# Second feed-forward of a two-layer step: the half products of the down projection woven in a written order, its sums in a place of their own

## The chip, the cores and the metric

The kernel runs on one core of a Trainium2 chip. The metric is the device time of one execution in microseconds (us). Before the change it was 1540.76 us, the median of three runs (1539.7 to 1543.07). One further execution was recorded by the hardware profiler: it took 1538.41 us, of which the instructions span 1536.6 us. All readings of the trace below are of that execution.

Engines are named as the profile names them: PE is the matrix engine, PEld its weight loads, DVE, ACT and POOL the vector, scalar and GpSimd engines, SP the engine that issues most loads.

## The reference, cut to what matters

The program computes one step through two trunk layers on 640 tokens (512 latent, 128 context) of width 1024. Layer 0 mixes the tokens by neighbourhood attention, layer 1 by a gated linear recurrent unit; each is followed by a SwiGLU feed-forward, and every part adds its result to the residual x through a gate vector:

```python
def _swiglu(x, w_gu, w_down):
    gate, up = jnp.split(x @ w_gu, 2, axis=-1)
    return (jax.nn.silu(gate) * up) @ w_down
```

The change lies in the second of the two feed-forwards. There `x @ w_gu` gives 22 units of 128 gate and 128 up columns (the hidden width is 2816), and `w_down` takes the 2816 hidden values back to eight rows of 128. Everything is float32.

## The kernel before, in words

**Arithmetic.** A float32 product is made of three matmuls on rounded halves: high weight by high data, high weight by low data, low weight by high data (lines 1208 to 1210 in `product`, 258 to 260 in `chunk`). So every weight tile and every data tile exists as a high part, cast by ACT (line 1668), and a low part, subtracted by DVE (line 1669). A matmul here is 128x128 by 128x320, since the 640 tokens are taken in two halves of 320 columns.

**Seven products in place of eight.** The second feed-forward treats a pair of output rows and the two halves of the tokens as a 2x2 block product and makes it from seven half products: A11·B11, A12·B21, S2·T2, S1·T1, S3·T3, A22·T4 and S4·B22. A are blocks of the weights, S sums of such blocks, B blocks of the data and T sums of those. Several products add up in one PSUM bank, one after the other: A11·B11, then S2·T2, S3·T3 and A22·T4 go into one bank ("mx"), S1·T1 and S4·B22 into a second ("mc" or "at"), A12·B21 has a third ("mm"). Between two products on a bank its value is copied out to SBUF by ACT, because it is a partial result that another output needs: this copy is called a snapshot ("snap", line 1214 for the gate products, line 1316 for the down products, where it also scales by the gate vector). PE can't write the next product into the bank until the snapshot is read out.

**Stages.** `ffn_halves` goes through the units of the hidden width. Two are plain and their down projection is done by `project_first` (96 matmuls, eight rows of 640 tokens, scaled into the tile of x and added to the residual in DRAM by eight POOL transfers of 320 KB that add in memory). The other 20 go in five chunks of four. A unit's gate and up columns are one pair of seven products, 84 matmuls, in `pair_a` (A11·B11, A12·B21), `pair_b` (S2·T2, S1·T1, S3·T3) and `pair_c` (A22·T4, S4·B22). DVE then multiplies gate and up and `hidden_sums` makes the data blocks B11, B21, B22 and T1 to T4 of the down product from the hidden values; part of them lies in a wide tile ("big"), part in the tile of x. After each of the first four chunks follows `down`: four pairs of output rows, seven products of six matmuls each, 168 matmuls. Its 16 results per chunk are 128x320 pieces of 160 KB, added to the residual in DRAM by POOL transfers (`add_x`); they are written into four places in SBUF (two called "sq", one "ssq", one "dg"), in turn. The last chunk is projected by `project_last`, after the residual is loaded back, and the final norm follows.

**Weights.** `down_weights` loads one pair's block, casts and subtracts the high and low parts, makes S1 to S4 on DVE (line 1298) in one of two places called "sum", and splits those too. POOL makes the same sums of the gate weights (line 1179) in the same two places. Weight halves are "whi"/"wlo" (from A) and "whx"/"wlx" (from S), three places of each.

**What sets the order.** Inside this feed-forward the order on each engine is made by a scheduler, which simulates the program and takes what it holds to be ready first; each instruction then waits for its inputs and for the places it writes. `in_order` (line 1672) pins engines to the order in which the code is written; before the change the second feed-forward doesn't use it. `ORDERED[:1]` is PE alone.

Of the kernel before, what the change touches and what calls it, by code (L numbers as in the profile page):

```python
# [50 lines left out]
PS = 4  # L51
BLK = ((0, 0), (0, 1), (1, 1), (1, 0))
# [90 lines left out]

class _Step:
    def __init__(self, ctx, nc, tc, i, o):
# [3 lines left out]
        self.n, self.ng, self.nu, self.hold, self.late = 0, 0, 0, None, []  # L149
# [491 lines left out]
    def project_last(self, w, hi, lo, gk):  # L641
# [26 lines left out]
        def square(f):  # L668
            q[f] = self.ssq[:, b0:b1] if f == 0 else self.t([P, HT], F32, "snap", 3, self.sb)[:, 0:b1 - b0]
            nc.scalar.activation(q[f], x[:, f, b0:b1], AF.Square)  # L670
# [14 lines left out]
        def final(k0, k1, t0, t1, r):  # L685
            v = x[:, k0:k1, t0:t1]
            nc.vector.tensor_tensor(v, v, r.unsqueeze(1).broadcast_to([P, k1 - k0, t1 - t0]), ALU.mult)
            nc.sync.dma_start(self.o["y"][k0 * P:k1 * P, t0:t1].rearrange("(k p) t -> p k t", p=P), v)
# [523 lines left out]
    def snap(self, ps):  # L1212
        s = self.t([P, HT], F32, "snap", 3, self.sb)
# [16 lines left out]
    def lay_hidden(self):  # L1230
        x = self.t([P, KT, NTOK], F32R, "x", 1, self.xp).rearrange("p k t -> p (k t)")
# [3 lines left out]
        spots += [(x, c * n) for c in range(6)] + [(t, c * n) for c in range(2) for t in self.wide]  # L1235
# [34 lines left out]

    def project_first(self, w, gk, xd):
        nc = self.nc
        G = self.need(self.gcols, gk)
        x = self.t([P, KT, NTOK], F32, "x", 1, self.xp)
        for f in range(0, KT, 2):
            for j, u in enumerate(self.two(w[f:f + 2], False)):
                o = x[:, f + j]
                for t0, t1 in CH:
                    ps = self.chunk(u, self.hhi, self.hlo, t0, t1, False)
                    for s, a, b in _pieces(t0, t1):  # L1280
                        g = G[:, s, f + j:f + j + 1]
                        if t0:
                            nc.vector.tensor_scalar(o[:, a:b], ps[:, a - t0:b - t0], g, None, ALU.mult)
                        else:
                            nc.scalar.activation(o[:, a:b], ps[:, a - t0:b - t0], AF.Copy, scale=g)
                self.add_x(xd, f + j, 0, o)

    def down_weights(self, i, d):
# [5 lines left out]
        s = self.t([P, 4, PS // 2 * P], F32, "sum", 2, self.sb)  # L1294
# [10 lines left out]
    def down(self, i, gk, xd):  # L1305
        nc, H = self.nc, self.H
        G = self.need(self.gcols, gk)
        W, b, c, u2, turn = {}, {}, {}, {}, count()

        def out():  # L1310
            tag = ("sq", "ssq", "sq", "dg")[next(turn) % 4]
            return self.t([P, HT], F32, tag, 1 + (tag == "sq"), self.sb)
# [6 lines left out]
        def snap(ps, f, t0):  # L1319
            return scaled(self.t([P, HT], F32, "snap", 3, self.sb), ps, f, t0)  # L1320
# [498 lines left out]
```

## Time and profile before

| what | us |
|---|---|
| median of three runs | 1540.76 |
| profiled execution | 1538.41 |
| span of its instructions | 1536.6 |
| PE busy in the span | 1485.3 (97%) |
| DVE busy | 1138.3 (74%) |
| ACT busy | 789.4 (51%) |
| POOL busy | 310.9 (20%) |
| start of the second feed-forward, two plain units and first chunk | 1057.0 to 1148.5 |
| first, second, third and fourth `down` | 1148.5 to 1187.8, 1238.3 to 1278.0, 1328.5 to 1369.0, 1419.7 to 1460.0 |

The profile counts PE as busy from a matmul's issue to its modelled end, at whatever clock was granted, so a high share does not say that PE ran at its full rate. The rate is seen from the number of matmuls in a stretch. The view of stretches prints for each stretch its length, then busy us and instruction count of PE, PEld, DVE, ACT and POOL, the granted PE clock as a share of the full one, the busy share of the DMA engines and GB/s. The view of waits lists whom an engine waited for, the total, the number of times and the longest time. In a timeline the bracket at a row's end gives the engine's idle time before it and what ended it.

### The profile page before, as it was taken

The page shows a single profiled execution, that of the slowest core. Times are in us where ns is not written, and L with a number is a line of the kernel's source. Part 1 is how long each engine was busy: PE and PEld are TensorE (multiplying, and loading weights), DVE is VectorE, ACT ScalarE, POOL GpSimd, SP SyncE. Part 2 cuts the span into 40 slices and gives each one's busy share as a digit, 9 for nine tenths or more (in the row PEclk, how much of TensorE's full clock was granted, in tenths as well). Part 3 has the DMA queues.
Part 4 walks back from the last instruction along what each step waited for, and adds up shares of the span by engine and source line. Part 5 has one row for each costly group of instructions (what it writes and reads, how often), then busy time and mean ns, then how long its engine had stood idle before and what let it go on. Part 6 is the DMA issues. An engine that isn't in the chain of part 4 may idle for free.

```text
span 1536.6 us, 26655 instructions
## 1 busy us (share of the span) xinstructions
PE 1485.3 (97%) x10281; PEld 1436.7 (93%) x10281; DVE 1138.3 (74%) x2166; ACT 789.4 (51%) x1489; POOL 310.9 (20%) x397
## 2 busy tenths in 40 slices
PE   9999999999999999999999999999988989898897
PEld 5999999899999999999999999999988979788797
DVE  6778787875777789878864799858684866759465
ACT  5667666754343244223343788646454544445454
POOL 0100000000022322112100011120515335152421
PEclk9999999999999999999999999999999999899999
DMA  9555555252478999778746442571636263453641
GB/s 359 187 164 168 150 165 167 68 192 83 137 241 318 343 345 333 254 248 269 257 144 203 169 152 96 209 244 56 138 106 100 83 118 89 115 91 101 107 149 69
DMA packets 94287, 268.50 MB, mean 175 GB/s; under 512 B 10144, under 2 KB 30800, under 8 KB 94032
## 3 DMA queue, kind: packets, MB, share of 16 engines
q1 hardware_dynamic: 57040, 157.06, 30.6%
q0 software_dynamic: 36944, 109.60, 24.8%
q8 instruction: 81, 1.33, 0.3%
q14 instruction: 46, 0.38, 0.1%
q10 hardware_dynamic: 176, 0.13, 0.0%
HBM read 206.18 MB, written 56.64 MB: 171 GB/s over the span
## 4 chain that ended last, share of the span: by engine, by line
PE 78%; DVE 7%; DMA 6%; ACT 4%; issue 2%; POOL 2%; DVEq 0%; SPq 0%; POOLq 0%; ACTq 0%
PE mm L260 11%; PE mm L259 11%; PE mm L258 11%; PE mx L258 5%; PE mx L260 5%; PE mx L259 5%; PE mx L1208 3%; PE mx L1209 2%; PE mx L1210 2%; PE op L893 2%; DMA sw<-in_wm 2%; DMA raw<-in_ds 2%; PE gp L1551 2%; PE tp L811 2%; POOL sum L1179 2%
## 5 line engine op out<-in xcount | busy, mean ns | idle before, releaser
L259 PE MATMUL mm<-big,whi 128*128 128x320 f32 (+2 forms) x754 | 234.2, 311 | 0.3 <-DVE big L1669 0.3
L260 PE MATMUL mm<-big,wlo 128*128 128x320 f32 (+2 forms) x754 | 234.0, 311 | 0.0
L258 PE MATMUL mm<-big,whi 128*128 128x320 f32 (+2 forms) x754 | 233.3, 312 | 0.0
L297 DVE SCALAR_TENSOR_TENSOR mprod<-mraw,csb 128x1024 f32<-128x1024 f32 x160 | 194.7, 1217 | 12.3 <-DMA mraw<-in_wm 11.7
L1668 ACT CAST whi<-raw 128x1024 fp32r<-128x1024 f32 (+3 forms) x103 | 101.9, 991 | 108.9 <-PE mm L259 51.0
L1669 DVE TENSOR_TENSOR wlo<-raw,whi 128x1024 fp32r<-128x1024 f32 (+3 forms) x103 | 119.8, 1164 | 43.3 <-ACT whi L1668 42.9
L259 PEld LDWEIGHTS mm<-big,whi 128*128 128x128 f32 x754 | 142.4, 189 | 1.7 <-DVE big L1669 0.5
L260 PEld LDWEIGHTS mm<-big,wlo 128*128 128x128 f32 x754 | 142.1, 189 | 1.0
L258 PEld LDWEIGHTS mm<-big,whi 128*128 128x128 f32 x754 | 141.8, 189 | 1.2
L260 PE MATMUL mm<-big,wlx 128*128 128x320 f32 (+3 forms) x443 | 137.2, 310 | 0.0
L259 PE MATMUL mm<-big,whx 128*128 128x320 f32 (+3 forms) x443 | 137.1, 310 | 0.0
L258 PE MATMUL mm<-big,whx 128*128 128x320 f32 (+3 forms) x443 | 137.0, 309 | 0.0
L293 POOL DMA_DIRECT2D mraw<-in_wm x80 | 42.9, 537 | 312.8 <-DVE mprod L297 209.2
L258 PE MATMUL mx<-big,whi 128*128 128x320 f32 (+2 forms) x318 | 99.0, 312 | 0.0
L260 PE MATMUL mx<-big,wlo 128*128 128x320 f32 (+2 forms) x318 | 98.4, 310 | 0.0
L259 PE MATMUL mx<-big,whi 128*128 128x320 f32 (+2 forms) x318 | 98.2, 309 | 0.0
L260 PEld LDWEIGHTS mm<-big,wlx 128*128 128x128 f32 x443 | 83.6, 189 | 0.0
L259 PEld LDWEIGHTS mm<-big,whx 128*128 128x128 f32 x443 | 83.5, 189 | 0.0
L258 PEld LDWEIGHTS mm<-big,whx 128*128 128x128 f32 x443 | 83.4, 188 | 0.0
L1669 DVE TENSOR_TENSOR wlx<-sum,whx 128x1024 fp32r<-128x1024 f32 x56 | 70.8, 1265 | 9.7 <-ACT whx L1668 8.7
L260 PE MATMUL mx<-big,wlx 128*128 128x320 f32 (+3 forms) x229 | 71.1, 311 | 0.0
L259 PE MATMUL mx<-big,whx 128*128 128x320 f32 (+3 forms) x229 | 71.0, 310 | 0.0
(457 smaller groups left out, 4428.7 us busy)
## 6 DMA issues: line engine op xcount, KB each, us to landing
raw<-in_gu SPq DMA_DIRECT2D x84, 512.0 KB, 3.7
mraw<-in_wm POOLq DMA_DIRECT2D x80, 512.0 KB, 5.2
sw<-in_wm SPq DMA_DIRECT2D x16, 512.0 KB, 10.8
raw<-in_wqk SPq DMA_DIRECT2D x16, 512.0 KB, 4.5
mraw<-in_wi POOLq DMA_DIRECT2D x16, 512.0 KB, 6.4
kwi<-kwh POOLq DMA_DIRECT2D x16, 512.0 KB, 6.0
kwi<-kwl POOLq DMA_DIRECT2D x16, 512.0 KB, 5.7
raw<-in_ds SPq DMA_DIRECT2D x16, 512.0 KB, 3.5
```

The source lines that it names most:

```text
L258: nc.tensor.matmul(ps, hi[:, k], xhi[:, k, s], start=(k == 0), stop=False)
L259: nc.tensor.matmul(ps, hi[:, k], xlo[:, k, s], start=False, stop=False)
L260: nc.tensor.matmul(ps, lo[:, k], xhi[:, k, s], start=False, stop=(k == nk - 1))
L293: nc.gpsimd.dma_start(w, self.i["wm"][l * 6 + j - 2, f])
L297: nc.vector.scalar_tensor_tensor(prod, w, 1.0, self.csb[:, s], ALU.mult, ALU.mult, accum_out=out[:, s, f:f + 1])
L811: turn = nc.tensor.transpose(tp[:, j * P:j * P + P], s[:, j * P:j * P + P], self.ident)
L893: mm = nc.tensor.matmul(out, v, w, start=start, stop=stop)
L1179: (nc.vector if vector else nc.gpsimd).tensor_tensor(*o)
L1208: nc.tensor.matmul(ps, hi[:, k], xh[:, k], start=start and k == 0, stop=False, skip_group_check=not start)
L1209: nc.tensor.matmul(ps, hi[:, k], xl[:, k], start=False, stop=False, skip_group_check=not start)
L1668: high = self.nc.scalar.copy(hi, v).ins
L1669: return high, self.nc.vector.tensor_tensor(lo, v, hi.bitcast(F32), ALU.subtract).ins
```

## The change

The seven products of a pair of output rows become seven steps with letters: a is A11·B11, b is A12·B21, c is S2·T2, d is S1·T1, e is S3·T3, f is A22·T4, g is S4·B22; W is a pair's weights; a digit names the pair of rows. `down` now runs a written list of steps in which two pairs alternate, and PE is pinned to it. The end of the chunk's last unit and the beginning of the next chunk's first unit are in the same list, ahead of, between and behind the steps.

Beside that: S1 to S4 of the down weights go to a single place of their own ("dsum"), which is a part of the tile of x; that tile is cut into three parts ("x0", "x2", "x4") so that each can be had by itself. There are four snapshots in place of three, and the one behind step a has two further places. `project_first` comes later, after the first pieces of the second pair of products, and writes its results in 16 pieces of 160 KB through the four result places in place of eight of 320 KB from the tile of x. The scaling and storing of the final output is cut along the parts of x, which adds one multiplication and one store. No matmul is added or removed.

```diff
     def down_weights(self, i, d):
...
-        s = self.t([P, 4, PS // 2 * P], F32, "sum", 2, self.sb)
+        s = self.dsum
...
     def lay_hidden(self):
-        x = self.t([P, KT, NTOK], F32R, "x", 1, self.xp).rearrange("p k t -> p (k t)")
+        xa, x = [self.t([P, b - a, NTOK], F32R, "x%d" % a, 1, self.xp).rearrange("p k t -> p (k t)") for a, b in (XS[0], XS[2])]
+        self.dsum = self.t([P, 4, PS // 2 * P], F32, "x%d" % XS[1][0], 1, self.xp)
...
+    def out(self):
+        self.turn += 1
+        tag = ("sq", "ssq", "sq", "dg")[self.turn % 4]
+        return self.t([P, HT], F32, tag, 1 + (tag == "sq"), self.sb)
+
     def project_first(self, w, gk, xd):
...
-                    ps = self.chunk(u, self.hhi, self.hlo, t0, t1, False)
+                    ps, o = self.chunk(u, self.hhi, self.hlo, t0, t1, False), self.out()
...
-                self.add_x(xd, f + j, 0, o)
+                    self.add_x(xd, f + j, t0, o)
...
+        def a(d):
+            bank[d] = self.ps("mx")[:, 0:HT]
+            self.product(bank[d], W[d]["A11"], "B11", True, H)
+            s1[d] = scaled(self.t([P, HT], F32, "c22", 2, self.sb), bank[d], 2 * d, 0)
+
+        def b(d):
+            ps = self.pg(False)[:, 0:HT]
+            self.product(ps, W[d]["A12"], "B21", True, H)
+            both(ps, s1[d], 2 * d, 0)
+
+        def s(d):
+            self.product(bank[d], W[d]["S2"], "T2", False, H)
+            u2[d] = snap(bank[d], 2 * d, HT)
+
+        def d_(d):
+            c[d] = (self.ps(("at", "mc")[d % 2]) if d < 3 else self.pg(False))[:, 0:HT]
+            self.product(c[d], W[d]["S1"], "T1", True, H)
+
+        def e(d):
+            self.product(bank[d], W[d]["S3"], "T3", False, H)
+            both(c[d], snap(bank[d], 2 * d + 1, HT), 2 * d + 1, HT)
+
+        def f(d):
+            self.product(bank[d], W[d]["A22"], "T4", False, H)
+            self.add_x(xd, 2 * d + 1, 0, scaled(self.out(), bank[d], 2 * d + 1, 0))
+
+        def g(d):
+            self.product(c[d], W[d]["S4"], "B22", False, H)
+            both(c[d], u2[d], 2 * d, HT)
+
+        def run(order):
+            for step in order.split():
+                dict(a=a, b=b, c=s, d=d_, e=e, f=f, g=g, W=weights)[step[0]](int(step[1]))
+
+        run("W0")
+        qs.append(self.gate_weights(l, f0))
+        qn = qs[f0]
+        for sums in self.s_sums(qn):
+            sums(False)
+        with self.in_order(ORDERED[:1]):
+            self.pair_b(qs[f0 - 1], j, False)
+            run("W1")
+            self.pair_a1(qn)
+            self.pair_c(qs[f0 - 1])
+            self.pair_a2(qn)
+            self.last_weights(qn)
+            run("W2 a0 d0 a1 d1 c0 c1 b0 e0 e1 b1 f0 f1 W3 g0 g1")
+            self.s_split(qn, 0)
+            run("a2 d2 c2 a3 d3 b2 e2 c3 b3 f2 e3 g2")
+            self.s_split(qn, 1)
+            self.pair_b1(qn)
+            run("f3 g3")
+            self.pair_b2(qn, 0, whole)
```

How the order moves, at three places.

On PE, first `down`, the first pair of output rows, before (each row stands for one product, of which the first matmul is shown; "x" and "big" hold the data sums, "whi" weights A, "whx" weight sums S; "mx" is the pair's first bank):

```order
L1208 MATMUL mx_13893<-x_12472,whx_13874 128x320
...
L1208 MATMUL mx_13893<-big_11721,whx_13874 128x320
...
L1208 MATMUL mx_13893<-big_11721,whi_13865 128x320
...
L1208 MATMUL at_13921<-x_12472,whx_13874 128x320
...
L1208 MATMUL mm_14114<-x_12472,whi_14072 128x320
```

and the same place after:

```order
L1223 MATMUL mx_13920<-x_1991_12263,whx_13754 128x320
...
L1223 MATMUL mx_13936<-x_1991_12263,whx_13825 128x320
...
L1223 MATMUL mm_13970<-x_1990_12262,whi_13746 128x320
...
L1223 MATMUL mx_13920<-big_11723,whx_13754 128x320
...
L1223 MATMUL mx_13936<-big_11723,whx_13825 128x320
...
L1223 MATMUL mm_14006<-x_1990_12262,whi_13817 128x320
...
L1223 MATMUL mx_13920<-big_11723,whi_13746 128x320
...
L1223 MATMUL mx_13936<-big_11723,whi_13817 128x320
```

Before, steps c, e and f of a pair follow each other directly on one bank; now at least one product on another bank, six matmuls, stands between any two of them.

On DVE, second `down`, from the product of gate and up of the chunk's last unit (line 1254) to the low half of T2 (the last row), before:

```order
L1254 TENSOR_TENSOR g_14544<-mx_14516,g_14544 128x320
L1669 TENSOR_TENSOR wul_14740<-raw_14723,wuh_14739 128x512
L1298 TENSOR_TENSOR sum_14764<-sum_14764,raw_14758 128x256
L1669 TENSOR_TENSOR x_12472<-g_14544,x_12472 128x320
L1298 TENSOR_TENSOR sum_14764<-raw_14758,sum_14764 128x256
L1669 TENSOR_TENSOR wlo_14871<-raw_14868,whi_14870 128x768
...
L1326 SCALAR_TENSOR_TENSOR sq_14789<-mm_14782,G_1502_8353,snap_14780 128x320
...
L1250 TENSOR_TENSOR r_12473<-g_14708,r_12473 128x320 x2
...
L1669 TENSOR_TENSOR x_12472<-r_12473,x_12472 128x320
```

and after:

```order
L1270 TENSOR_TENSOR g_14563<-mx_14535,g_14563 128x320
L1719 TENSOR_TENSOR wul_14779<-raw_14640,wuh_14778 128x512
L1317 TENSOR_TENSOR x_1992_12264<-raw_14782 128x256 x2
L1234 TENSOR_TENSOR g_14747<-mc_14662,snap_14660 128x320
...
L1719 TENSOR_TENSOR wlo_14785<-raw_14782,whi_14784 128x768
L1270 TENSOR_TENSOR g_14747<-c_2403_14689,g_14747 128x320
L1266 TENSOR_TENSOR r_12265<-g_14747,r_12265 128x320 x2
L1719 TENSOR_TENSOR wlx_14793<-x_1992_12264,whx_14792 128x1024
...
L1719 TENSOR_TENSOR x_1991_12263<-r_12265,x_1991_12263 128x320
```

DVE's weight work stands in the same stretch as before, in another order; the first result of `down` (line 1326) has moved behind T2.

On POOL, the additions of `project_first`, before:

```order
L1269 DMA xd<-x_12303 128x640 x2
...
L1269 DMA xd<-x_12303 128x640 x4
...
L1269 DMA xd<-x_12303 128x640
...
L1269 DMA xd<-x_12303 128x640
```

and after (the first nine of 16):

```order
L1285 DMA xd<-ssq_12413 128x320
L1285 DMA xd<-dg_12434 128x320
L1285 DMA xd<-sq_12423 128x320
...
L1285 DMA xd<-sq_12444 128x320
L1285 DMA xd<-ssq_12461 128x320
L1194 TENSOR_TENSOR sum_12674<-sum_12674,raw_12635 128x512
L1285 DMA xd<-sq_12471 128x320
L1285 DMA xd<-dg_12482 128x320
L1285 DMA xd<-sq_12492 128x320
```

They have moved among POOL's sums of gate weights, are twice as many, and each place is used four times.

More of the change, by code (lines that the diff above doesn't have):

```diff
@@ L1 @@
 from contextlib import ExitStack, contextmanager, nullcontext
-from itertools import count
 import numpy as np
@@ L141, in _pieces, with __init__, cuts, __getitem__ @@
     return [(s, max(a, t0), min(b, t1)) for s, a, b in ((0, 0, NLAT), (1, NLAT, NTOK)) if max(a, t0) < min(b, t1)]
+class _Parts:
+    def __init__(self, tiles):
+        self.tiles = tiles
+    def cuts(self, k0, k1):
+        return [(max(a, k0), min(b, k1)) for a, b, _ in self.tiles if max(a, k0) < min(b, k1)]
+    def __getitem__(self, i):
+        p, k, *rest = i
+        first = k.start if isinstance(k, slice) else k
+        a, _, t = next(v for v in self.tiles if v[0] <= first < v[1])
+        return t[(p, slice(k.start - a, k.stop - a) if isinstance(k, slice) else k - a, *rest)]
 class _Step:
@@ L1303, in down_weights, with down @@
         return W
-    def down(self, i, gk, xd):
+    def down(self, i, l, gk, xd, qs, j, f0, whole):
         nc, H = self.nc, self.H
         G = self.need(self.gcols, gk)
[L1308 to L1312, printed above, removed]
+        W, bank, c, s1, u2 = {}, {}, {}, {}, {}
         def scaled(o, ps, f, t0):
@@ L1327, in both, with weights @@
             self.add_x(xd, f, t0, o)
[L1329 to L1330 removed]
+        def weights(d):
             W[d] = self.down_weights(i, d)
[L1332 to L1356 removed]
@@ L1358, in pair_a @@
-    def pair_a(self, q, whole=True):
-        W = q["W"]
-        q["b"] = b = self.ps("mx")[:, 0:HT]
-        self.product(b, W["A11"], "B11", True)
-        s1 = self.snap(b)
-        a = self.pg(False)[:, 0:HT]
-        self.product(a, W["A12"], "B21", True)
-        q["g1"] = self.total(a, s1, "g") if whole else (a, s1)
+        def a(d):
+            bank[d] = self.ps("mx")[:, 0:HT]
+            self.product(bank[d], W[d]["A11"], "B11", True, H)
+            s1[d] = scaled(self.t([P, HT], F32, "c22", 2, self.sb), bank[d], 2 * d, 0)
@@ new lines, in pair_a1, with pair_a2, pair_b1 @@
+    def pair_a1(self, q):
+        q["b"] = b = self.ps("mx")[:, 0:HT]
+        self.product(b, q["W"]["A11"], "B11", True)
+        q["s1"] = self.snap(b)
+    def pair_a2(self, q, whole=True):
+        a = self.pg(False)[:, 0:HT]
+        self.product(a, q["W"]["A12"], "B21", True)
+        q["g1"] = self.total(a, q["s1"], "g") if whole else (a, q["s1"])
+    def pair_a(self, q, whole=True):
+        self.pair_a1(q)
+        self.pair_a2(q, whole)
+    def pair_b1(self, q):
+        self.product(q["b"], q["W"]["S2"], "T2", False)
+        q["u2"] = self.snap(q["b"])
@@ L1367, in pair_b, with pair_b2 @@
     def pair_b(self, q, j, whole):
+        self.pair_b1(q)
+        self.pair_b2(q, j, whole)
+    def pair_b2(self, q, j, whole):
         W, b = q["W"], q["b"]
-        self.product(b, W["S2"], "T2", False)
-        q["u2"] = self.snap(b)
         q["c"] = c = self.ps("mc")[:, 0:HT]
```

96 lines of the change are left out of this document (34 added, 62 removed).

## The prediction

> **What bounds the kernel now.** First the page's engine totals, then the stretches of the second feed-forward beside one stretch in which PE runs without a gap, then whom PE waits for.
>
> ```profile
> PE 1485.3 (97%) x10281; PEld 1436.7 (93%) x10281; DVE 1138.3 (74%) x2166; ACT 789.4 (51%) x1489; POOL 310.9 (20%) x397
> ```
>
> ```profile
> 920.00:960.00 40.00, 40.00 (x273) 40.00 (x272) 37.19 (x54) 34.99 (x56) 4.97 (x5) 1.00 0.32 105
> 1057.00:1148.50 91.50, 85.32 (x560) 83.46 (x558) 73.94 (x127) 47.66 (x89) 29.54 (x26) 0.98 0.42 110
> 1148.50:1187.80 39.30, 33.56 (x189) 30.25 (x190) 18.25 (x37) 17.25 (x35) 17.87 (x19) 0.91 0.64 103
> 1238.30:1278.00 39.70, 33.92 (x192) 30.61 (x193) 18.82 (x37) 17.33 (x35) 18.27 (x19) 0.91 0.61 102
> 1328.50:1369.00 40.50, 34.70 (x190) 31.26 (x191) 18.50 (x37) 17.34 (x36) 18.03 (x19) 0.87 0.61 100
> 1419.70:1460.00 40.30, 34.57 (x197) 31.13 (x198) 19.44 (x38) 17.26 (x35) 18.58 (x20) 0.92 0.64 107
> ```
>
> PE bounds the program: 97% busy. The undisturbed stretch has 273 matmuls in 40 us, so one costs 40/273 = 0.1465 us. The four stretches around `down` issue 192 each by the program (168 of `down`, 24 of the gate units; the records differ by a few) and would take 192 x 0.1465 = 28.1 us at that pace. They take 39.3, 39.7, 40.5 and 40.3, together 159.8; 159.8 - 112.5 = 47.3 us are lost, 11.8 in each. DVE is busy half of these stretches and ACT less, so neither is short of time: what is lost is order.
>
> ```profile
> PE mx L1208 <- ACT snap L1316: 17.9, 32, 0.8
> PE mx L1208 <- ACT x L1668: 5.5, 4, 1.4
> PE mx L1209 <- DVE x L1669: 4.2, 4, 1.0
> PE mc L1208 <- DVE c L1219: 2.3, 4, 1.1
> ```
>
> These are PE's waits from 1060 us to the end. The first row is 32 waits of 0.56 us on `down`'s snapshots, eight in each `down`. Rows two and three are the high and low half of T2, once per `down`, (5.5 + 4.2)/4 = 2.4 us. Together 6.9 us of the 11.8. The next rows show the clock, in the third `down`:
>
> ```profile
> 1328.56 0.41 PE L1208 MATMUL mx<-x,whx 128*128 128x320 f32 x1 [1.43 <-ACT x L1668]
> 1330.01 0.63 PE L1209 MATMUL mx<-x,whx 128*128 128x320 f32 x1 [1.04 <-DVE x L1669]
> 1331.74 0.64 PE L1208 MATMUL mx<-big,whx 128*128 128x320 f32 x1 [0.83 <-ACT snap L1316]
> 1334.48 0.64 PE L1208 MATMUL mx<-big,whi 128*128 128x320 f32 x1 [0.77 <-ACT snap L1316]
> ```
>
> ```profile
> 1325.00:1330.00 5.00, 2.45 (x14) 1.70 (x12) 5.00 (x12) 2.19 (x5) 0.88 (x1) 0.96 0.46 108
> 1330.00:1335.00 5.00, 3.39 (x10) 2.59 (x11) 1.89 (x6) 1.82 (x6) 0.00 (x0) 0.50 0.32 105
> 1335.00:1340.00 5.00, 5.00 (x21) 5.00 (x20) 3.11 (x5) 2.31 (x3) 3.49 (x4) 0.51 0.70 79
> ```
>
> Four gaps of 1.43, 1.04, 0.83 and 0.77 us, 4.1 us within 6, and from 1330 on the granted clock stands near 0.50: 31 matmuls in 10 us. They would take 4.5 us; 1.6 us of gaps lie in these 10, so about 3.9 go with the clock here. The stretch's mean of 0.87 stands for (1 - 0.87) x 40.5 = 5.3 us of lost clock, the 0.91 of the first two for 3.6; at the same share, 3.9/5.3, the others lose 2.4 to 2.7. The mean of the four is about 2.9. With 6.9 that leaves 2.0 of the 11.8 for the gate units' waits and small gaps.
>
> The Trainium skill ("TensorE: Matmul & The Clock Gate", section "Why this matters for your kernels") asks for no PE gaps over some 3 us between bursts, as a full idle window brings the half clock. Here the longest single gap was 1.43 us and the clock halved: the trace doesn't agree, and decides. By the page alone the clock's loss would not come from gaps this short, its 2.9 us per `down` would stay, and the result below would be 11.6 us later, near 1521; a clock that stays low is part of the second rival.
>
> **Part one: the woven products.** c, e and f of a pair, which waited for a snapshot each, now have six matmuls of the other pair between them, 6 x 0.1465 = 0.88 us.
>
> ```profile
> L1316 ACT ACTIVATE snap<-mx,G 128x192 f32<-128x192 f32 x30 | 12.6, 421 | 60.9 <-PE mx L1210 60.9
> L1316 ACT ACTIVATE snap<-mx,G 128x128 f32<-128x128 f32 x30 | 10.8, 360 | 0.0
> L1326 DVE SCALAR_TENSOR_TENSOR sq<-mm,G,snap 128x320 f32<-128x320 f32 x14 | 7.7, 549 | 0.0
> L1668 ACT CAST whi<-raw 128x1024 fp32r<-128x1024 f32 x16 | 16.8, 1048 | 12.2 <-DMA raw<-in_gu 6.8 <-PE mx L1209 5.4
> ```
>
> A snapshot's two pieces take 0.42 and 0.36, together 0.78, and the longest wait for one was 0.83: the 0.88 covers it where ACT is free to read out at once. The cover is another product; were the pairs not alternating, 0.56 would be due at each. What remains I count per `down`.
>
> T2. Its chain on DVE begins with gate times up of the chunk's last unit and ends with T2's low half:
>
> ```profile
> 1320.40 0.48 DVE L1254 TENSOR_TENSOR g<-mx,g 128x320 f32<-128x320 f32 x1
> 1323.59 0.96 DVE L1669 TENSOR_TENSOR wlo<-raw,whi 128x768 fp32r<-128x768 f32 x1 [1.03 <-ACT whi L1668]
> 1324.87 1.22 DVE L1669 TENSOR_TENSOR wlx<-sum,whx 128x1024 fp32r<-128x1024 f32 x1
> 1329.47 0.48 DVE L1669 TENSOR_TENSOR x<-r,x 128x320 fp32r<-128x320 f32 x1
> ```
>
> From 1320.40 to 1329.95 that is 9.5 us, in which PE had 42 matmuls to issue, 6.2 us. The new order has 48 there (S4·B22, A12·B21 of the next unit, a0, d0, a1, d1), 7.0 us. DVE's instructions in the new chain, added up at the distances between starts in this stretch (0.40 for 320 columns, 0.60 for 512, 0.34 for a 256-column sum, 0.88 for 768, 1.14 for 1024), make 8.0; with some 1.0 of waiting for casts, as at 1323.59, 9.0. So the wait falls from 2.4 by 0.8 and 0.5 to about 1.1; I take 1.4, since ACT's cast of T2's high half lies in the chain. Bounds: 0, when the casts are early, and 2.9, when all is as now.
>
> The result places. The woven order asks for eight results in about 7 us (b0, e0, e1, b1, f0, f1, g0, g1), before it came one in 2.5. There are four places, and one comes free when its transfer has landed:
>
> ```profile
> xd<-sq POOLq DMA_DIRECT2D x32, 160.0 KB, 4.1
> xd<-x POOLq DMA_DIRECT2D x8, 320.0 KB, 8.4
> xd<-ssq POOLq DMA_DIRECT2D x16, 160.0 KB, 3.4
> xd<-dg POOLq DMA_DIRECT2D x16, 160.0 KB, 3.9
> ```
>
> The time to landing counts from the issue. With the 0.55 to 0.78 of writing and up to 1 us until POOL issues, a place is taken for near 5.5 us (an estimate from these rows): four places give one result per 1.4 us, not eight in 7. Here is a new wait: ACT's write of f0 stands until b0's result has landed, DVE's of g0 until e1's has. Behind f0 on ACT stand f1, a weight cast and the snapshot of a2; behind g0 on DVE the reading out that frees the bank "at" for d2; PE waits for both at the seam between the two woven halves. Counted from b0's end at 0, with 0.88 a product: f0's product is done at 3.5, its place comes free at 5.5; f1, a cast of 1.05 and a2's snapshot follow until near 8.5, and c2 would have started at 7.9: 0.6 lost. e1's place comes free near 7.4 and g0's read-out ends near 7.9, when d2 would have started at 7.0: 0.9. Together 1.5 us. Bounds: 0, when landings take the 3.3 of the shortest row below, and 5, when each of four turns is late by as much again.
>
> Small waits (the first matmuls on a new bank, the last snapshot): 1.0, two of the eight snapshot waits of 0.56. Four gaps no longer fall within 6 us: they are 1.4 and then 1.5 some 8 us later; I take the clock as granted, which removes the 2.9. Left: 1.4 + 1.5 + 1.0 = 3.9 per `down`, 15.6; gain 47.3 - 15.6 = 31.7 us. "dsum" is one place where there were two: the sums of the next pair wait for ACT's cast and DVE's subtraction of the last. DVE has 20 idle us of 40 to hide it; I cost it at nothing. If ACT's cast comes late, DVE stands in front of the sums with T1 to T4 behind it: that is the second rival.
>
> **Part two: gate units.** The order of the last unit's pieces and the next unit's is fixed too. The waits on gate totals (the fourth row of waits, 2.3 us in four) and their like come where S3·T3 and A22·T4, or S4·B22 and the next S1·T1, follow each other on one bank. By counting such neighbours in both orders, at 0.65 to 0.75 each, I get 2.2 us a chunk before and 1.4 now (each kind once), in three chunks: gain 2.4. Bounds: 0 and 4.
>
> **Part three: `project_first`.** Its 16 results take the four places too. 16 at 1.4 us are 22 us; the matmuls with which they are woven number 181 in the new order, 26.5 us. So the places nearly suffice, but PE's "mm" banks stand until ACT and DVE have drained them, and those now wait for landings; where before a 320 KB transfer from the tile of x stopped nobody.
>
> ```profile
> DMA to landing us min/median/max: 5.7/8.4/10.1
> DMA to landing us min/median/max: 3.3/3.6/4.8
> ```
>
> First row the 320 KB transfers of this stretch, second the 160 KB ones in the second `down`. I take a loss of 3: three of 16 results late by a microsecond. Bounds: -2 (the moved gate products give PE more to do while DVE is behind in this stage, where it is busy 73.9 of 91.5 us) and +8 (each second result late by 1). **Part four: the end.** One more scaling and store, 0.2.
>
> **The sum.** -31.7 - 2.4 + 3.0 + 0.2 = -30.9. Against the profiled execution's 1538.41 (1.8 around the span) that is 1507.5; it lay 2.35 under the median, from which I count: 1540.76 - 30.9 = 1509.9, said as 1510.
>
> **Rivals.** *First: nearly all goes.* Landings as short as the least row (3.3) and DVE ahead: 0.8 left per `down` in place of 3.9, 4 x 3.1 = 12.4 less: 1497.5. For it: DVE's and ACT's idle halves. Against: the chain to T2 is longer than its cover by every count.
>
> *Second: T2 stays late.* POOL's sums of gate weights run close to the down block, and DVE's work slows beside them:
>
> ```profile
> L1250 DVE TENSOR_TENSOR g<-g,r 128x320 f32<-128x320 f32 x6 | 6.2, 1035 | 0.0
> L1250 DVE TENSOR_TENSOR r<-g,r 128x320 f32<-128x320 f32 x12 | 5.3, 484 | 0.1
> ```
>
> Two subtractions alike, one at 1035 ns in place of 484, and POOL is busy in the stretch with sums. Three of those in the chain add 1.6, the T2 wait is 2.9, and gaps follow so closely that the half clock (2.9) stays: 1.5 + 2.9 = 4.4 each, 17.6 in all: 1527.5. The rows show the slowing; against it, POOL's sums are now placed ahead of the chain. The Trainium skill ("SBUF — State Buffer", section "Who interferes with whom") says that a DVE instruction with two SBUF inputs contends with a GpSimd instruction that reads SBUF; these rows agree, 1035 against 484.
>
> *Third, the other side: the four places decide.* Five stages of four turns each (`project_first` and four `down`) would last 20 x (L + 1.5) us with a landing of L. They now take 159.8 + 26.5 = 186.3; the T2 waits (5.6) and parts two and four (-2.2) are beside it, so the point is 20 x (L + 1.5) = 182.9, L = 7.6 us. At the 8.4 of the 320 KB row it is 198.0 + 3.4 - 186.3 = +15.1: 1555.9. For it: results in bursts, twice the transfers in the first stage. Against: 3.3 to 4.8 in the second `down`, where POOL issued 16 such in 40 us.
>
> *Fourth: it doesn't do what it says*: PE's order changes but each wait comes back elsewhere: 1540.8. The order on PE is pinned, so only the length of waits can do that.
>
> **How the numbers follow.** Forecast 0.62, first rival 0.14, second 0.15, third 0.06, fourth 0.03. What a measurement can tell from no change is about 0.2%, 3.1 us. Faster: the first three, 0.91; the same 0.03; slower 0.06. The range holds the forecast with its bounds, the second rival and part of the first: 1496 to 1529, for 8 in 10.
>
> **What would show it.** Right: the four stretches of 192 matmuls at about 32 us each, PE's waits on `down`'s snapshots at under 4 us in all instead of 17.9, the clock at 0.97 or more there, a T2 wait of 1 to 2 us per `down`, and ACT or DVE waiting for landings at f0 and g0. In the first stage waits of ACT and DVE on landings, and PE 3 us later. Wrong: a clock still at 0.9 in the stretches (second rival); T2's wait under 0.5 (first); landings of over 6 us (third).

## The result, and the profile after

The changed kernel took 1532.32 us, the median of four runs (1531.29 to 1532.75), against 1541.19 for the kernel before in the same comparison (1539.7 to 1543.07). The ratio is 0.9941, with a 95% interval of 0.9924 to 0.9958: 8.9 us faster, where 31 were forecast and the range ended at 1529. The profiled execution took 1532.58 us with a span of 1530.8, 5.8 under the span before: the profiled execution of the kernel before lay 2.8 under its median in this comparison, so the traces show 6 of the 8.9 us.

The waits of PE in the second feed-forward after the change (whom it waited for, us in total, times, longest):

```profile
PE mc L1223 <- DVE g L1234: 22.8, 8, 4.4
PE at L1223 <- DVE dg L1341: 4.7, 4, 1.5
PE mx L1224 <- DVE x L1719: 4.6, 4, 1.2
PE mm L1225 <- DVE wlx L1719: 4.1, 4, 2.1
PE mx L1223 <- ACT snap L1229: 3.1, 6, 0.6
```

The 17.9 us on `down`'s snapshots are gone from the list. T2's wait (third row) is 1.2 us a `down`, the seam on the result places (second row) 1.2. But the first row is new. S1·T1 of a gate unit waits for DVE to add up the gate total from the bank "mc" into which S4·B22 of the unit before was put: 22.8 us in eight times, where the like before was 1.3 in four:

```profile
PE mc L1208 <- DVE g L1219: 1.3, 4, 0.6
```

The eight are of two kinds. Four stand at the chunk ends, 4.0 to 4.4 us each, where S1·T1 follows S4·B22 directly. Three stand in the middles, 2.0 to 2.2 each, with the 12 matmuls of S2·T2 between the two products (the eighth is under 0.2).

Both programs issue the same number of matmuls, so one can ask at what time each has issued its n-th. The recorded matmuls of both traces were lined up with the programs' orders for that; "chunk end" are the 84 matmuls ahead of the first step a of each `down`, "`down`" the 192 from there on, "middle" the 228 up to the next chunk end. Where a kernel's order on PE differs, the same count holds partly other products.

| us, in order of the chunks | before | after | difference |
|---|---|---|---|
| start, from 1072.0 us, 320 matmuls | 53.0 | 51.7 | -1.3 |
| chunk end, 84 each | 14.6, 14.3, 14.4, 14.5 | 19.5, 19.0, 19.0, 19.0 | +18.8 |
| `down`, 192 each | 39.8, 40.1, 41.4, 40.1 | 32.3, 32.2, 32.4, 35.2 | -29.3 |
| middle, 228 each | 35.4, 35.6, 35.4 | 37.5, 37.6, 37.4 | +6.2 |
| behind the last `down`, 292 | 46.0 | 45.6 | -0.4 |

The stretches of the second `down` after the change and of the chunk end ahead of it, and the same matmuls before (columns as in the prediction):

```profile
1213.10:1232.10 19.00, 15.00 (x85) 14.75 (x85) 14.97 (x25) 7.30 (x13) 4.02 (x3) 0.82 0.29 87
1232.10:1264.30 32.20, 29.22 (x195) 28.24 (x194) 21.36 (x42) 18.69 (x38) 14.47 (x16) 1.00 0.63 109
```

```profile
1214.80:1229.10 14.30, 13.00 (x86) 12.38 (x86) 11.83 (x22) 7.00 (x13) 2.72 (x2) 1.00 0.22 73
1229.10:1269.10 40.00, 33.80 (x193) 30.52 (x192) 24.95 (x50) 18.09 (x35) 15.64 (x17) 0.91 0.62 119
```

In `down` the clock went from 0.91 to 1.00 and 8 us are gone, as forecast. At the chunk end the clock went from 1.00 to 0.82, and 5 us are lost. The gain was made where it was forecast, and most of it given back just ahead of it.

What DVE and POOL did at that place, and the matmul that waited, from the timeline after:

```profile
1211.91 1.18 DVE L1266 TENSOR_TENSOR g<-g,r 128x320 f32<-128x320 f32 x1
1213.01 1.58 DVE L1719 TENSOR_TENSOR x<-r,x 128x320 fp32r<-128x320 f32 x1
1214.51 1.56 DVE L1719 TENSOR_TENSOR big<-r,big 128x320 fp32r<-128x320 f32 x1
1215.99 0.48 DVE L1234 TENSOR_TENSOR g<-mm,snap 128x320 f32<-128x320 f32 x1
1216.39 1.35 DVE L1719 TENSOR_TENSOR wul<-raw,wuh 128x512 fp32r<-128x512 f32 x1
...
1218.47 0.48 DVE L1234 TENSOR_TENSOR g<-mc,snap 128x320 f32<-128x320 f32 x1
```

```profile
1211.34 1.40 POOL L1194 TENSOR_TENSOR sum<-raw 128x512 f32<-128x512 f32 x1 [11.46 <-DVE wlx L1719]
...
1215.80 1.40 POOL L1194 TENSOR_TENSOR sum<-raw,sum 128x512 f32<-128x512 f32 x1
```

```profile
1219.00 0.64 PE L1223 MATMUL mc<-big,whx 128*128 128x320 f32 x1 [4.00 <-DVE g L1234]
```

PE had finished S4·B22 at 1215.0. DVE came to read it at 1218.47, since the work ahead of it in its queue took two to three times its usual time while POOL made the sums of the next unit's gate weights. Four rows, of 1.18, 1.58, 1.56 and 1.35, take 0.49, 0.49, 0.49 and 0.69 elsewhere: 3.5 us more together, and 3.5 us is how late DVE came. The row that reads PSUM (`g<-mm,snap`) took its 0.48 among them.

The waits in the middles have another cause. There DVE stood for the load of the first pair's down weights, with the read-out behind it:

```profile
1203.47 0.76 DVE L1317 TENSOR_TENSOR x<-raw 128x256 f32<-128x256 f32 x2 [2.76 <-DMA raw<-in_ds]
```

### The profile page after: what moved, and what is told of

Read it like the earlier page. It is cut to its first block, busy times and chain, and to the rows that moved or that the text cites. A ratio compares the mean times of both kernels' runs of the same rounds, so it can differ in the third digit from the quotient of the medians.

```text
span 1530.8 us, 26689 instructions
## 1 busy us (share of the span) xinstructions
PE 1475.0 (96%) x10281; PEld 1435.8 (94%) x10281; DVE 1134.6 (74%) x2167; ACT 789.2 (52%) x1489; POOL 316.6 (21%) x405
## 5 line engine op out<-in xcount | busy, mean ns | idle before, releaser
L272 PE MATMUL mx<-big,whi 128*128 128x320 f32 (+3 forms) x322 | 100.5, 313 | 1.5 <-ACT whi L1718 1.1
L274 PE MATMUL mx<-big,wlo 128*128 128x320 f32 (+3 forms) x322 | 99.7, 310 | 0.0
L273 PE MATMUL mx<-big,whi 128*128 128x320 f32 (+3 forms) x322 | 99.7, 310 | 0.0
L1223 PE MATMUL mc<-big,whx 128*128 128x320 f32 x168 | 55.7, 332 | 23.7 <-DVE g L1234 22.8
L237 ACT CAST kwh<-mraw 128x1024 fp32r<-128x1024 f32 x33 | 34.6, 1049 | 73.4 <-DMA kwi<-kwh 30.6
```

What stands on the lines that cost most here:

```text
L237: nc.scalar.copy(high, raw)
L272: nc.tensor.matmul(ps, hi[:, k], xhi[:, k, s], start=(k == 0), stop=False)
L273: nc.tensor.matmul(ps, hi[:, k], xlo[:, k, s], start=False, stop=False)
L274: nc.tensor.matmul(ps, lo[:, k], xhi[:, k, s], start=False, stop=(k == nk - 1))
L1223: nc.tensor.matmul(ps, hi[:, k], xh[:, k], start=start and k == 0, stop=False, skip_group_check=not start)
```

## The experiments

Of each kernel the edit is shown against the changed kernel, if nothing else is said. The table behind the runs gives the same stretches for all. The runs with fills leave the sums of the gate weights out.

**Two banks.** Is it the bank?

```diff
-            c[d] = (self.ps(("at", "mc")[d % 2]) if d < 3 else self.pg(False))[:, 0:HT]
+            c[d] = self.cbank() if d < 3 else self.pg(False)[:, 0:HT]
...
+    def cbank(self):
+        self.cturn = 1 + getattr(self, "cturn", 0)
+        return self.ps(("at", "mc")[self.cturn % 2])[:, 0:HT]
...
-        q["c"] = c = self.ps("mc")[:, 0:HT]
+        q["c"] = c = self.cbank()
```

> The gate units' second bank alternates between two PSUM banks (mc and at), unit by unit; the down steps take the same turn. Theory A (PE stands in the gate units because S1·T1 wants the one bank that S4·B22 has just filled, and DVE reads it out late): the row of PE's waits on DVE's gate totals, 22.8 us in 8, falls under 4 us, the granted clock around the chunk ends comes back from 0.83-0.95 to near 1.0, and part of DVE's lateness returns at T2 (1.2 us before, up to 4): 1510 to 1520 us. Theory B (DVE itself is late, since it stands for the load of the first pair of down weights): the waits only move from this bank to the next thing that DVE owes PE, 1528 to 1533. Theory C (POOL's sums slow DVE): as B.

1541.23 us, ratio to the kernel before 1.0008 (0.9992 to 1.0025): slower than the change. PE's waits:

```profile
PE mx L1223 <- ACT snap L1229: 21.0, 16, 4.1
PE mx L1223 <- ACT x L1722: 6.3, 4, 1.7
```

The wait on the bank is gone, the chunk ends fall from 76.5 to 53.7 us and their clock is back at 1.00, as theory A said, but the time does not follow. T2 waits 2.4 us a `down` in place of 1.2, and the new first row holds three waits of 3.9 to 4.1 in the middles, where S3·T3 stands for ACT's snapshot. That copy was queued behind casts of down weights, for whose load ACT had stood:

```profile
1204.89 0.83 ACT L1722 CAST whi<-raw 128x768 fp32r<-128x768 f32 x1 [4.55 <-DMA raw<-in_ds]
...
1208.68 0.42 ACT L1229 COPY snap<-mx 128x320 f32<-128x320 f32 x1
```

```profile
1209.15 0.42 PE L1223 MATMUL mx<-big,whx 128*128 128x320 f32 x1 [3.92 <-ACT snap L1229]
```

So PE did stand on the bank at the chunk ends, and a second one takes that away, but the time is lost elsewhere: the middles take 12.7 us more and `down` 11.8. That DVE was late behind all of these waits is not shown by this run.

**The first pair's weights later.** The wait of DVE for the load of the first pair's weights (2.76 us at 1203.47) is moved away. The second pair's weights come later too.

```diff
-        run("W0")
         qs.append(self.gate_weights(l, f0))
...
-            run("W1")
+            run("W0")
             self.pair_a1(qn)
             self.pair_c(qs[f0 - 1])
             self.pair_a2(qn)
             self.last_weights(qn)
-            run("W2 a0 d0 ...
+            run("W1 W2 a0 d0 ...
```

> The first pair's down weights are loaded, cast and summed after the last gate unit's S2·T2, S1·T1 and S3·T3 instead of ahead of them, the second pair's after the next unit's first products. Theory A: only the 2.1 us wait ahead of the last unit goes in three chunks, the 4.0 us one stays at 3.4 or more: 1525 to 1529. Theory B: with DVE 2.8 us earlier the 4.0 falls near 1.3 and the clock holds, (2.1 + 2.7 + 2.5) x 3 = 22 us: 1508 to 1514. If the pair's weights now come too late for the first down product, a wait of PE on them appears instead: 1530 or more.

1537.33 us, ratio 0.9978 (0.9965 to 0.9991). The chunk ends fell from 76.5 to 58.6 us in sum, but the middles rose by 11.6 and `down` by 9.7: the waits went to snapshots (15.5 us) and to the seam (8.1). The waits of 2.1 in the middles are gone, so they were the load's. The largest new ones, 3.3 in each chunk but the first, stand just ahead of the chunk end: A22·T4 waits for a snapshot that ACT makes behind casts of hidden sums, and the two DVE subtractions before those casts took 2.93 us beside POOL's sums, against 0.88 in the change. Theory B, that the load's delay is all of it, falls; moving the weights pays nothing.

**Fills in place of POOL's sums.**

```diff
-                    (nc.vector if vector else nc.gpsimd).tensor_tensor(*o)
+                    nc.vector.tensor_tensor(*o) if vector else nc.gpsimd.memset(o[0], 0.01)
```

> Leaves out the sums S1 to S4 of the gate weights in the second feed-forward: POOL fills their places with a constant instead, so it reads nothing from SBUF; all else is done. Theory C (DVE is slowed by POOL reading): DVE's 320-column subtractions of 1.2 to 1.6 us at the chunk ends fall to 0.48, 4.3 us per chunk, the 4.0 us waits go: 1505 to 1515. Theory A without C: the slowing is no cause, DVE is late by the order of its queue: 1526 to 1533.

1503.96 us (one run). In the second to fourth chunk the order of PE through the chunk end and its `down` is the same as in the change, S1·T1 still right behind S4·B22; parts of the start and of the middles have another order. The wait on gate totals:

```profile
PE mc L1223 <- DVE g L1234: 3.0, 4, 1.2
```

Without POOL's sums the time is some 6 us under what was forecast of the change. Two things went together here, though: a fill doesn't read, and it doesn't hold the raw weights until the sum is made, so loads come earlier.

**No pin.**

```diff
-        with self.in_order(ORDERED[:1]):
+        with nullcontext():
```

> The same written code, but PE is not pinned to it in the four down blocks. Theory D (the pin itself places S1·T1 right behind S4·B22): the scheduler puts other products between, the gate waits of 22.8 us fall under 8, while some snapshot waits of down return (up to 8 us in all): 1516 to 1524. If the adjacency comes from the order of the code and not from the pin: waits as they are, 1530 to 1535.

1518.06 us, ratio 0.985 (0.9833 to 0.9866): 14 us faster than with the pin, as theory D had it. PE's wait on the gate totals:

```profile
PE mc L1223 <- DVE g L1234: 7.7, 4, 3.1
```

In the free order the next unit's A11·B11 and A12·B21 and step a0 of `down` stand ahead of S1·T1, and PE has them to do while DVE is late.

**The kernel before with fills** (the same edit on the kernel before).

> The kernel before, with POOL's sums of gate weights left out and replaced by fills with a constant, as in the fills run on the change (1504 us). Theory: the slowing of DVE by POOL's reading hurts PE only where PE's order gives it nothing else to do, and before the change the free order hid most of it: 1530 to 1538, a gain of 3 to 10 against the 28 on the change. Rival: POOL's reading costs the same anywhere, the order of PE has no part in it: 1508 to 1516.

1544.65 us, ratio 1.003 (1.0008 to 1.0052): slower, outside both expectations. The scheduler made another order with the fills, and a wait appeared that the kernel before doesn't have:

```profile
PE mx L1208 <- ACT snap L1316: 13.8, 24, 0.8
PE mm L1208 <- ACT whi L1668: 13.1, 4, 3.7
```

The waits on gate totals are nearly gone (0.5 us), but 13.1 us on a weight cast came in. So this run doesn't say what POOL's reading costs in the order before.

**No pin, with fills.**

> The change without the pin on PE and with fills in place of POOL's sums of gate weights (left out). Theory (pin and slowing hurt together, each is cheap alone): 1500 to 1506, as with the pin and fills (1504), while without fills the pin costs 14. Rival (the pin costs the same with or without the slowing): 1488 to 1492.

1501.34 us (two runs). With the pin POOL's sums make a difference of 28 us (1532 against 1504), without it 17 (1518 against 1501); the pin makes 14 with the sums and 3 with the fills. They hurt together, as the theory had it, but the sums are not cheap alone. The order of PE differs between the two runs without the pin (at 1464 of 10281 places by the names of the tiles), so the 17 are not the slowing's alone.

**Fills of equal length** (each sum two fills).

> As the first fills run on the change, with the pin, but each of POOL's sums of gate weights is replaced by two fills of 0.6 us, which keep POOL about as long (1.2 against 1.4 us) and hold the raw weights as long. The sums are left out. Theory (it is DVE's slowing by POOL's reading): 1503 to 1509. Rival (it is that the fills end earlier, so that loads and casts come earlier): 1518 to 1532.

1504.06 us (two runs). POOL was busy 74.5 us with fills of 607 ns in the feed-forward, about twice the first fills' 38.5 (the sums of the change took 107.6), and it changed nothing: that POOL is busy is not the cause. That raw places come free earlier is not excluded by it, since a fill doesn't read the raw weights and so can't hold them, unlike what the expectation says.

**The pin on `down` alone.**

```diff
-        with self.in_order(ORDERED[:1]):
-            self.pair_b(qs[f0 - 1], j, False)
+        self.pair_b(qs[f0 - 1], j, False)
...
+        with self.in_order(ORDERED[:1]):
             run("W2 a0 d0 a1 d1 c0 c1 b0 e0 e1 b1 f0 f1 W3 g0 g1")
...
-            self.pair_b1(qn)
             run("f3 g3")
-            self.pair_b2(qn, 0, whole)
+        self.pair_b1(qn)
+        self.pair_b2(qn, 0, whole)
```

> PE is pinned to the written order only for down's own steps; the last unit of a chunk and the first of the next stand outside the pin in the code. Theory (the harm is in pinning the gate products, down's weave is good): 1511 to 1519, gate waits of DVE under 9 us as without any pin, down's snapshot waits under 2. Rival (any pin on down costs what a gate product could have filled): 1522 to 1532.

1538.38 us, ratio 0.9999 (0.9987 to 1.0012): the theory missed by 19. The gate waits are as short as without any pin, but `down` is long, 152.9 us for its four stretches:

```profile
PE mc L1223 <- DVE g L1234: 8.7, 7, 2.7
PE mx L1223 <- ACT snap L1229: 7.0, 9, 2.6
PE mx L1223 <- ACT x L1718: 5.5, 4, 2.1
PE mc L1223 <- DVE sq L1341: 5.5, 3, 2.3
PE at L1223 <- DVE dg L1341: 5.1, 4, 1.4
```

The free gate products are put among the pinned steps, and waits of 1 to 2.5 us on five different things follow. Which of them drew the others was not tried.

**One unit's sums by DVE.**

```diff
-            sums(False)
+            sums(True)
```

> The change with the pin; the four sums of a chunk's next unit are made by DVE instead of POOL. DVE gets 2.7 us of work in the same place and loses the slowing there, 4.3 us. Theory (the slowing decides): a little faster than the change, 1524 to 1530. Rival (DVE's amount of work decides, not its slowing): slower than the change, 1535 to 1545.

1529.38 us (two runs), ratio 0.9929 (0.9909 to 0.9948), within the theory's 1524 to 1530. The interval overlaps that of the change, so the times alone do not separate the two. The order of PE is the same, matmul for matmul, and its waits on gate totals are 20.2 us in place of 22.8: DVE does 2.7 us more there and is still a little earlier.

**POOL's sums behind T2.**

```diff
-        for sums in self.s_sums(qn):
-            sums(False)
+        late = self.s_sums(qn)
...
             self.pair_c(qs[f0 - 1])
+            mark = nc.gpsimd.tensor_copy(..., H["T2l"][:, 1, 0:1].bitcast(F32)).ins
+            for sums in late:
+                with self.tc.issue_after(mark):
+                    sums(False)
```

> The change, with PE pinned and its order at the chunk ends as in the change, and all work done; only POOL's four sums of the next unit's gate weights are queued behind T2's low half (a one-column copy on POOL that reads it stands ahead of them). Theory (POOL reading SBUF while DVE makes the hidden sums is what makes DVE late, and S1·T1 behind S4·B22 on one bank exposes it): DVE's 320-column operations there back at 0.48, the gate waits on DVE fall from 22.8 to under 8; the later sums hold raw places, so the third and fourth pair's weights come 1 to 3 us late in a down: 1512 to 1522. Rival (the gain of the fills was that the sums' time itself went): 1528 to 1538.

1537.78 us, ratio 0.9993 (0.9976 to 1.0009): the time is the rival's, the mechanism is not. PE's order is that of the change, matmul for matmul by the names of the tiles. At the same place, DVE's rows and the matmul that waits:

```profile
1213.95 0.49 DVE L1266 TENSOR_TENSOR g<-g,r 128x320 f32<-128x320 f32 x1
1214.35 0.49 DVE L1722 TENSOR_TENSOR x<-r,x 128x320 fp32r<-128x320 f32 x1
1214.75 0.49 DVE L1722 TENSOR_TENSOR big<-r,big 128x320 fp32r<-128x320 f32 x1
...
1218.61 0.49 DVE L1234 TENSOR_TENSOR g<-mc,snap 128x320 f32<-128x320 f32 x1 [1.47 <-PE mc L1225]
```

```profile
1219.15 0.41 PE L1223 MATMUL mc<-big,whx 128*128 128x320 f32 x1 [0.58 <-DVE g L1234]
```

1.18, 1.58 and 1.56 us have become 0.49 each, DVE now waits for PE, and PE's 4.00 us are 0.58. The chunk ends take 53.8 us in place of 76.5, at a clock of 1.00. Here all work is done and raw places are held longer, not shorter: that the slowing makes the loss at the chunk ends is shown. The waits of 2.1 in the middles stay. But `down` lost 30 us, and POOL's rows say why:

```profile
1241.78 1.29 POOL L1194 TENSOR_TENSOR sum<-raw,sum 128x512 f32<-128x512 f32 x1
1243.01 0.88 POOL L1285 DMA_DIRECT2D xd<-ssq  x1
1243.60 1.19 POOL L1285 DMA_DIRECT2D xd<-sq  x1
1244.14 1.54 POOL L1285 DMA_DIRECT2D xd<-dg  x1
1244.68 1.89 POOL L1285 DMA_DIRECT2D xd<-sq  x1
```

```profile
PE at L1223 <- DVE dg L1341: 14.7, 4, 5.5
PE mx L1223 <- ACT ssq L1331: 11.8, 4, 4.2
PE mc L1223 <- DVE g L1234: 9.9, 7, 2.2
```

The four sums stand ahead of the transfers of the first four results in POOL's queue. None of the four places can come free before the first transfer is issued at 1243.0, the next results wait, and PE waits at the seam: 26.5 us in all, where the change had 4.7.

**The same without the pin** (both edits).

> The same without the pin on PE. Theory (both together expose it, either cure is enough for most): 1508 to 1516, less than either cure's own gain added (1518 without pin alone). Rival (the cures add up): 1500 to 1506.

1524.96 us, ratio 0.9906 (0.9885 to 0.9927): worse than the free order alone, outside both expectations; `down` takes 144.6 us in place of 136.5. In the second `down` POOL's sums stand ahead of result transfers here too, and DVE waits 3.3 and 3.7 us for landings, but PE's waits on results stay under half a microsecond. PE stands at T2 instead (gaps of 1.28, 0.74 and 0.65 us), and the clock is 0.90 or 0.91 in all four, against 0.90 to 0.95 in the free order. What draws these gaps together was not tried.

**`project_first` where it was.**

```diff
-        self.lay_hidden()
         self.pair_b(q, 0, False)
+        self.project_first(self.i["dn"][l, :, :, 0:PLAIN], (l, 5), xd)
+        self.lay_hidden()
...
-                if f == PLAIN + 1:
-                    self.project_first(self.i["dn"][l, :, :, 0:PLAIN], (l, 5), xd)
```

> The change, but the two plain units' down projection stands where it stood before the change, ahead of the hidden sums' places; it still writes 16 results through the four places. Tells the price of the third part. If the four places cost 3 us as predicted and the later position costs nothing: 1532 as the change. If the later position is what gained (the start of the stage is 4 us ahead of before in the change's trace, with no loss to landings): 3 to 6 us slower than the change, 1535 to 1539.

1539.95 us, ratio 0.9998 (0.9986 to 1.0011), a microsecond beyond the second expectation. The start takes 58.1 us, against 51.7 in the change and 53.0 before. Its waits on results in this stage:

```profile
PE mm L272 <- DVE sq L1302: 2.6, 1, 2.6
PE mm L272 <- ACT dg L1304: 1.5, 1, 1.5
```

So with the four places `project_first` is some 5 us slower at its old position, 4.1 of them in these two waits, and the later one, where gate products lie between, takes that back and a little more.

**Cover inside the pin.** PE stays pinned, and the written order gives it the work that the free order had found:

```diff
-            self.pair_b(qs[f0 - 1], j, False)
-            run("W1")
+            self.pair_b1(qs[f0 - 1])
             self.pair_a1(qn)
-            self.pair_c(qs[f0 - 1])
             self.pair_a2(qn)
+            self.pair_b2(qs[f0 - 1], j, False)
+            run("W1")
+            self.pair_c(qs[f0 - 1])
```

> PE stays pinned, POOL makes the sums as in the change; in the written order the next unit's A11·B11 and A12·B21 are moved ahead of the last unit's S1·T1, so that other products lie between it and S4·B22 on the same bank (ten matmuls right between, 24 in all ahead of S1·T1). Theory (the pin's 14 us against the free order is this: PE had work it could have done while DVE was late): the 4.0 us waits fall to 1 or less, the clock holds, T2 waits 1 to 2 us longer since 12 matmuls less lie ahead of it: 1514 to 1522. Rival (DVE's lateness comes back in full at T2 or at snapshots, as with two banks): 1528 to 1540.

1522.65 us, ratio 0.9882 (0.9859 to 0.9905): 10 of the pin's 14 us, a little outside the theory's 1514 to 1522. The chunk ends fall to 60.4 us, `down` and the middles rise by 2.8 each. PE's waits:

```profile
PE mc L1223 <- DVE g L1234: 9.8, 5, 2.6
PE mx L1223 <- ACT snap L1229: 8.4, 10, 1.9
```

7.0 of the 9.8 us are the three waits in the middles, which the cover doesn't touch.

**Cover, and one unit's sums by DVE** (both edits).

> As the cover run, and the chunk's next unit's four sums are made by DVE instead of POOL (POOL doesn't read there). If the two cures work on the same wait: 1512 to 1520, within 4 us of the cover run. If slowing costs beyond that wait: 1504 to 1511.

1516.98 us, ratio 0.9842 (0.9812 to 0.9872), within the first expectation's range, but 5.7 us from the cover run where at most 4 were said. Its interval overlaps that of the cover run, so what the second cure adds to the first is not settled.

**No pin, and one unit's sums by DVE.**

> No pin on PE (1518 alone) and the chunk's next unit's sums on DVE (with the pin, 1529 against 1532). If DVE's 2.7 us of sums cost less than POOL's slowing here too: 1512 to 1517. If the free order had hidden the slowing: 1518 to 1522.

1513.24 us, ratio 0.9816 (0.9791 to 0.9841): the lowest median here of a kernel that does all the work, 27 us under the kernel before and 19 under the change. Its interval just overlaps that of the free order alone.

The stretches in the profiled executions (us; sums of four chunk ends, four `down`, three middles):

| kernel | start | chunk ends | `down` | middles | behind | median |
|---|---|---|---|---|---|---|
| before | 53.0 | 57.7 | 161.4 | 106.3 | 46.0 | 1541.2 |
| the change | 51.7 | 76.5 | 132.1 | 112.5 | 45.6 | 1532.3 |
| two banks | 55.2 | 53.7 | 143.9 | 125.2 | 50.9 | 1541.2 |
| first weights later | 51.8 | 58.6 | 141.8 | 124.1 | 45.7 | 1537.3 |
| fills | 49.9 | 52.1 | 133.2 | 108.0 | 44.2 | 1504.0 |
| fills of equal length | 50.0 | 52.2 | 128.5 | 115.2 | 44.0 | 1504.1 |
| before, fills | 53.9 | 49.4 | 159.5 | 115.8 | 50.4 | 1544.7 |
| no pin | 50.5 | 54.1 | 136.5 | 113.4 | 48.1 | 1518.1 |
| no pin, fills | 49.7 | 49.6 | 139.1 | 101.1 | 46.4 | 1501.3 |
| pin on `down` alone | 50.5 | 59.4 | 152.9 | 111.0 | 48.8 | 1538.4 |
| sums by DVE | 50.5 | 72.4 | 132.5 | 113.5 | 46.3 | 1529.4 |
| sums behind T2 | 50.8 | 53.8 | 162.5 | 115.9 | 46.7 | 1537.8 |
| the same, no pin | 49.7 | 49.5 | 144.6 | 113.3 | 48.6 | 1525.0 |
| `project_first` early | 58.1 | 72.8 | 134.5 | 113.3 | 46.9 | 1540.0 |
| cover | 49.8 | 60.4 | 134.9 | 115.3 | 47.3 | 1522.7 |
| cover, sums by DVE | 50.4 | 55.2 | 136.9 | 116.8 | 46.2 | 1517.0 |
| no pin, sums by DVE | 52.6 | 49.5 | 133.7 | 114.7 | 47.5 | 1513.2 |

The rows are of one execution each. Those of the sums behind T2, of cover with sums by DVE and of two banks took 5.8, 4.0 and 3.5 us more than their medians, that of sums behind T2 without the pin 4.8 less, that of before 2.8 less.

## Why the prediction was wrong

**Part one, `down`: right.** 31.7 us of gain were forecast and 29.3 came. T2 waits 1.2 us (1.4 said), "at" at the seam 1.2 (0.9 said); c2's 0.6 there didn't show. Not foreseen was a wait for a low half of weight sums (1.0 a `down`, 2.1 in the last, whose stretch is 35.2). The clock is at 1.00 in the first three and 0.95 in the last.

**Part two, the gate units: the step that failed.** The prediction counted the places where S4·B22 and the next S1·T1 "follow each other on one bank", at 0.65 to 0.75 us each, and forecast a gain of 2.4. That is the time of a read-out by a DVE with nothing else to do. At each chunk end such a place cost 4.0 to 4.4, and the clock fell with it: the chunk ends lost 18.8 us. (The other kind of neighbours, S3·T3 and A22·T4, cost 0.57, near what was said.) What stood ahead of the read-out in DVE's queue was not looked up, though the same walk had listed DVE's chain instruction by instruction for T2. A second wait, 2.0 to 2.2 in each middle, is no such neighbour and stood in the sum at nothing: the load of the first pair's weights keeps DVE from the read-out. The middles lost 6.2. In all 25.0 us were lost where 2.4 were to be gained; the term is off by 27.4, more than the whole miss of 22.4.

**The second rival named the cause and put it in the wrong place.** It had POOL's sums slowing DVE, as the two rows at 1035 and 484 ns showed, and gave 1527.5; but it held that T2 would wait longer. T2 did not (1.2 us): PE stood earlier, by enough that DVE had caught up by T2. The "point against" that POOL's sums are placed ahead of the chain was true and was the harm: they run beside the gate unit's work.

**What the free order hid.** Before the change DVE was slowed at the same place, on the same work:

```profile
1211.81 1.59 DVE L1250 TENSOR_TENSOR g<-g,r 128x320 f32<-128x320 f32 x1
1213.32 1.58 DVE L1669 TENSOR_TENSOR x<-r,x 128x320 fp32r<-128x320 f32 x1
```

The sum took the free order's waits on DVE at the chunk end (0.4 to 1.1 us) as the price of the same dependences. In it PE had other products to do just there (11 matmuls between S4·B22 and S1·T1 at this chunk end); the pin took them away. The cover run gives 10 us of that back inside the pin, the free order with the same code 14.

**Part three: the sign was wrong.** +3 forecast, -1.3 measured, inside the bounds and for the reason that the lower bound gave: the four places cost about 5 where `project_first` stood, the new position gains 6.4.

**The third rival**, the four places, didn't come in the change, where landings stay at 4.0 to 5.1 us; it came when POOL's queue was filled ahead of them (sums behind T2), by 26.5 us of waits.

**The signs.** Nearly all that was named as a sign of being right came: `down` at 32 us in three of four, its snapshot waits gone, T2's wait at 1.2, DVE and ACT standing for landings. The time was still wrong, since no sign looked at the chunk end. That the second rival's 1527.5 lies nearest to the measured time is luck: its late T2 and low clock in `down` didn't come.

What stays open: how the fills' 28 us divide. In the trace 24.4 of them lie at the chunk ends, where moving the sums gives 22.7 without any earlier release of raw weights; the rest, 4.5 in the middles above all, may be earlier loads or the other order there. Open too are what the pin on `down` alone set off, and what the sums behind T2 set off without the pin.

## What to carry to other kernels

A wait on a bank between two neighbouring products must be priced with what stands ahead of the read-out in the reading engine's queue at that moment (slowed work, a wait for a load), not with the read-out's own duration. Before an order is pinned, see what the free order had between each pair of dependent instructions, since that cover is lost without a trace in the list of waits. A cure that moves work to another place in a shared queue (here POOL's, which also issues the result transfers) has to be priced against what it now stands ahead of.

## What the runs showed of the hardware

A DVE subtraction of 128x320 with both inputs in SBUF took 893 ns in the mean in the change, 483 with POOL filling without reading; an addition with one input in PSUM took 480 and 487.

```profile
L1719 DVE TENSOR_TENSOR x<-r,x 128x320 fp32r<-128x320 f32 x8 | 7.1, 893 | 0.0
L1234 DVE TENSOR_TENSOR g<-mc,snap 128x320 f32<-128x320 f32 x20 | 9.6, 480 | 0.5 <-PE mc L1225 0.5
```

```profile
L1719 DVE TENSOR_TENSOR x<-r,x 128x320 fp32r<-128x320 f32 x8 | 3.9, 483 | 0.0
L1234 DVE TENSOR_TENSOR g<-mc,snap 128x320 f32<-128x320 f32 x20 | 9.7, 487 | 12.0 <-PE mc L1225 12.0
```

The first pair of rows is of the change, the second of the run with fills of equal length. The Trainium skill ("SBUF — State Buffer", section "Who interferes with whom") says that a DVE instruction with two SBUF inputs contends with a GpSimd instruction that reads SBUF, and not with one that only writes it. These rows agree with both halves.

The clock: a chunk end of 19 us with one gap of 4.0 us stood at 0.82, the same matmuls with one of 0.58 (sums behind T2) at 1.00. Gaps of 1.17, 1.10 and 0.67 us in the second `down`, spread over 15 us, left it at 1.00; before, four gaps of together 4.1 us within 6 us had halved it.
